# Stick-breaking attention: scores emitted two jobs ahead of their transposes, with six weight tiles and half the DMA scratch

## The chip, the core and the metric

The kernel runs on one core of a Trainium2 chip. A core has engines that run side by side, each with its own queue of instructions: PE (matrix products and transposes), DVE (element by element work and scans), ACT (activations and copies with a cast), POOL and SP (here mostly issues of transfers). The metric is the device time of one execution in microseconds, lower is better. The kernel has a median of 2229.0 us over three runs (2228.58 to 2229.59).

## The reference, cut to what matters

Two layers, each with two mixers on the same projected input; stick-breaking attention is the first of them. The rest (normalisation, compressed, selected and window attention, gates, output projection) is left out here.

```python
SEQ = 1024; DEPTH = 2; HEAD_DIM = 64; SB_HEADS = 8; Q_BLOCK = 128

def stick_breaking_attention(q, k, v):
    B, S, H, d = q.shape
    scale = d ** -0.5
    qh, kh, vh = (a.transpose(0, 2, 1, 3) for a in (q, k, v))
    outs = []
    for i in range(S // Q_BLOCK):
        t0, t1 = i * Q_BLOCK, (i + 1) * Q_BLOCK
        z = jnp.einsum('bhqd,bhkd->bhqk', qh[:, :, t0:t1], kh[:, :, :t1]).astype(jnp.float32) * scale
        strict = jnp.arange(t1)[None, :] < jnp.arange(t0, t1)[:, None]
        log_keep = jnp.where(strict, jax.nn.log_sigmoid(-z), 0.0)
        between = lax.cumsum(log_keep, axis=3, reverse=True) - log_keep
        w = jnp.where(strict, jnp.exp(jax.nn.log_sigmoid(z) + between), 0.0)
        outs.append(jnp.einsum('bhqk,bhkd->bqhd', w.astype(v.dtype), vh[:, :, :t1]))
    return jnp.concatenate(outs, axis=1)

# in the layer
a = stick_breaking_attention(heads(sb_q, SB_HEADS), heads(sb_k, SB_HEADS), heads(sb_v, SB_HEADS))
a = a.reshape(B, S, SB_WIDTH) * jax.nn.silu(sb_z)
y = jax.nn.sigmoid(m_a) * (a @ w_proj_a) + jax.nn.sigmoid(m_b) * (b @ w_proj_b)
return x + gate[:, None] * (y @ w_out)
```

## The kernel before

A layer runs `early` (projections that everything needs), then queues the remaining projections as a reserve of matrix products (`queue_projections`, the "fill"), then the sparse attention (`nsa`), then the stick-breaking stage `sb`, then what is left of the fill, then `output`. What the fill holds during `sb` are products for the gates: PE rows on lines 194, 196 and 198 with `proj` as their output, whose weights come from HBM as `raw` and are split into two parts `w` by ACT and DVE (lines 136, 137).

`sb(l)` goes over 8 heads, and in each over 4 jobs m = 0 to 3. Job m takes two tiles of 128 query rows, tile i = 2m + x with x = 0 and 1, against the first (i + 1) x 128 keys. So the widths are 128 and 256 for m = 0, 384 and 512 for m = 1, 640 and 768 for m = 2, 896 and 1024 for m = 3.

A job has a part A and a part B.

- Part A (`sb_scores`): for each chunk of up to 512 keys PE computes scores (lines 872, 873, and 875 for the mask), ACT makes C (the sigmoid of the negative score, line 1245) and E (the sigmoid of the score, line 1246), and after the last chunk DVE runs a reverse product scan over C (line 1249) and multiplies E by it (line 1250). E is then the tile of weights. Its pool has four buffers, C has three. POOL sets the border column of C.
- Part B (`pipeline`): PE transposes the two E tiles block by block (line 885, output `tr`), ACT casts the transposed block to `wh` (line 136), DVE takes the rest `wl` (line 137), and PE multiplies both with V into `av` (lines 904 and 905), three steps behind the transposes. At its end `merge` adds two halves (ACT `mt`, line 922; DVE `o`, line 923), and for odd heads `finish_pair` multiplies `o` with the gate (line 913) and stores it to AD in HBM (line 914).

`run_jobs` interleaves the pieces of part A of one job with those of part B of the job before. After each piece it pumps fill products worth a number of microseconds: `sb_us` = (1.34, 2.87, 4.77, 6.04) for the B job's m, in the first iteration, which has no B, `start_us` = 3.0. On each engine the emitted instructions are then ordered by a list scheduler, which follows the emission with small shifts, and each engine works through its own list in that order.

`load(head)` brings k (two transfers on SP's queue), V and q (on ACT's queue) into pools of two buffers. It is called at the beginning of B of (head - 1, 0). After `sb` the function `output` loads AD with transfers on POOL's queue (line 1339, three for each half of the rows; `actlo`, then split into `acthi`) and gates `gt` (line 1405). GpSimd's transfers keep their descriptors in a reserved part of SBUF, `dynamic_dma_scratch_size`, 16384 bytes of each partition where nothing is said.

Of the kernel before, what the change touches and what calls it, by code (L numbers as in the profile page):

```python
# [10 lines left out]
F32 = mybir.dt.float32  # L11
# [9 lines left out]
P = 128  # L21
S = 1024
# [65 lines left out]
class Trunk:  # L88
# [195 lines left out]
            self.run_gen(self.fill.pop(0)[1])  # L284
        self.debt = 0.0

    def run_jobs(self, jobs):


        for n in range(len(jobs) + 1):  # L290
            B = jobs[n - 1][1] if n else []
            A = jobs[n][0] if n < len(jobs) else []
            us = jobs[n - 1][2] if n else self.start_us
            merged = []
            for x in range(max(len(A), len(B))):
                merged += A[x:x + 1] + B[x:x + 1]
            for f in merged:
                f()
                self.pump(us * (1 - self.tail) / len(merged))
            self.pump(us * self.tail)  # L300
# [75 lines left out]
    def mod_ab(self, l, pool, steps):  # L376
# [3 lines left out]
        sc = self.sc  # L380
        B = self.tl(self.lay, [P, KD], F32, "Bcol", bufs=2)
        A = self.tl(self.lay, [P, KD], F32, "Acol", bufs=2)
        ab, gn = self.vectors(pool, l)
        self.mods[l] = (A, B)

        def fin(part, ps):
# [3 lines left out]
            else:  # L390
                nc.vector.tensor_tensor(B, ps, ab[:, 0], ALU.add)

# [58 lines left out]
    def norm_first(self):  # L451
# [3 lines left out]
        with tc.tile_pool(name="norm0", bufs=1, reuse_waits="tile") as pool:  # L455
            A = self.tl(self.lay, [P, KD], F32, "Acol", bufs=2)
            B = self.tl(self.lay, [P, KD], F32, "Bcol", bufs=2)
            ada = {}
# [724 lines left out]
    def sb(self, l):  # L1183
        tc, nc = self.tc, self.nc
        with tc.tile_pool(name=f"sb{l}", bufs=2, reuse_waits="tile") as pool:
            qkv = {}

            def load(head):
                if head >= 8:
                    return  # L1190
                k = self.load_stack_k(pool, 512 + head * 64)
                v = self.load_v(pool, head)
                q = self.tl(pool, [P, S], F32R, "q")
                for hl in range(2):
                    nc.scalar.dma_start(q[hl * 64:hl * 64 + 64].bitcast(F32), self.QK[hl, head * 64:head * 64 + 64, :])
                qkv[head] = (q, k, v)

            def job(head, m, st):
                hs = {}
                A, B = [], []  # L1200
                for x in range(2):
                    A += self.sb_scores(pool, m, x, lambda: qkv[head], hs)

                def begin():
                    if m == 0:
                        load(head + 1)
                    hs["ps"] = self.tl(self.pav, [P, 512], F32, "av", bufs=1)
                bursts = self.pipeline(pool, self.av_stages(pool, m, lambda: (hs["e", 0], hs["e", 1]),
                                                            lambda: qkv[head][2]), lambda: hs["ps"], True)
                B.append(lambda: (begin(), bursts[0]()))  # L1210
                B += bursts[1:]

                def fin():
                    if head % 2 == 0:
                        st[m] = self.tl(pool, [P, 256], F32, f"o{m}", bufs=1)
                    self.merge(pool, hs["ps"], st[m], head % 2)
                    if head % 2 == 1:
                        self.finish_pair(pool, st[m], head // 2 * 128, m, 512 + head // 2 * 128)
                B.append(fin)
                return A, B, self.sb_us[m]  # L1220

            load(0)
            jobs = []
            st = {}
            for head in range(8):
                for m in range(4):
                    jobs.append(job(head, m, st))
            self.run_jobs(jobs)

    def sb_scores(self, pool, m, x, qkv, hs):  # L1230

        nc = self.nc
        i = 2 * m + x
        nk = (i + 1) * P

        def chunk(c0):
            q, k, _ = qkv()
            if c0 == 0:
                hs["e", x] = self.tl(pool, [P, S], F32, "E", bufs=4)
                hs["c", x] = self.tl(pool, [P, S + 8], F32, "C", bufs=3)  # L1240
                nc.gpsimd.memset(hs["c", x][:, nk:nk + 1], 1.0)
            e, c = hs["e", x], hs["c", x]
            c1 = min(nk, c0 + 512)
            ps = self.scores(q[:, i * P:i * P + P], k, c0, c1, [(i * P, "m_strict")] if c1 == nk else [])
            nc.scalar.activation(c[:, c0:c1], ps, AF.Sigmoid, scale=-(HD ** -0.5))  # L1245
            nc.scalar.activation(e[:, c0:c1], ps, AF.Sigmoid, scale=HD ** -0.5)
            if c1 == nk:
                rev = c[:, nk - 1::-1]
                nc.vector.tensor_tensor_scan(rev, rev, rev, 1.0, ALU.mult, ALU.bypass)  # L1249
                nc.vector.tensor_tensor(e[:, 0:nk], e[:, 0:nk], c[:, 1:nk + 1], ALU.mult)  # L1250

        return [lambda c0=c0: chunk(c0) for c0 in range(0, nk, 512)]
# [206 lines left out]
```

## Time and profile before

| what | before |
|---|---|
| median of three runs | 2229.0 us (2228.58 to 2229.59) |
| time of the profiled execution | 2227.61 us |
| its span | 2225.8 us |
| PE busy | 2124.4 us (95%) |
| DVE busy | 1573.0 us (71%) |
| ACT busy | 1129.9 us (51%) |
| stick-breaking stage of layer 0, layer 1 | about 690 to 950 us, 1780 to 2040 us |

The span is the time between the first and the last instruction that the profile shows; the execution's own time is 1.8 us more. Busy time is the time in which an engine had an instruction in work; matmuls on PE are pipelined and their ends are modelled. In the waits an instruction stands with the engine that released it and the idle time ahead of it.

### The profile page before, as it was taken

What the parts mean: (1) busy time and instruction counts of PE and PEld (TensorE: products, weight loads), DVE (VectorE), ACT (ScalarE), POOL (GpSimd) and SP (SyncE); (2) the same over time, 40 slices, a digit from 0 to 9 for tenths busy, and PEclk for the clock granted to TensorE, in tenths of its full rate; (3) what the DMA queues carried; (4) which work ended last, traced back from release to release, by engine and by line L of the source; (5) the groups of instructions that cost most, each with busy time, mean ns of one, the idle gap of its engine ahead of it and who ended that gap; (6) DMA issues with size and microseconds to landing.
All of it is one profiled execution on the core that took longest, in us unless ns stands there. A gap on an engine that the chain in (4) does not pass through costs nothing.

```text
span 2225.8 us, 36846 instructions
## 1 busy us (share of the span) xinstructions
PE 2124.4 (95%) x13128; PEld 1833.5 (82%) x13128; DVE 1573.0 (71%) x3722; ACT 1129.9 (51%) x2489; POOL 73.0 (3%) x242
## 2 busy tenths in 40 slices
PE   4999999999999999999999998999999999999999
PEld 3898778988887777779889986889898877777899
DVE  5768558868765877886766852887788487787643
ACT  4433147656565655663433421665666465656410
POOL 2200000000000000010011000000000000001000
PEclk8999999999999999999999999999999999999999
DMA  7545852253116445275555355222522364534443
GB/s 287 113 136 189 251 154 81 91 152 94 64 48 159 128 130 129 81 245 177 164 151 161 107 192 141 90 90 82 146 92 68 97 151 113 146 98 166 148 124 104
DMA packets 254104, 297.05 MB, mean 133 GB/s; under 512 B 38888, under 2 KB 201568, under 8 KB 253920
## 3 DMA queue, kind: packets, MB, share of 16 engines
q1 hardware_dynamic: 213152, 250.65, 37.4%
q10 hardware_dynamic: 36224, 29.37, 5.1%
q0 software_dynamic: 4544, 14.68, 2.3%
q8 instruction: 103, 1.69, 0.3%
q14 instruction: 81, 0.66, 0.1%
HBM read 206.28 MB, written 83.89 MB: 130 GB/s over the span
## 4 chain that ended last, share of the span: by engine, by line
PE 66%; DVE 18%; DMA 7%; issue 4%; ACT 3%; POOL 1%; SPq 0%; ACTq 0%; DVEq 0%; POOLq 0%
PE proj L194 15%; PE proj L198 15%; PE proj L196 15%; PE tr L885 5%; DVE C L1249 4%; PE av L905 4%; PE av L904 3%; PE sc L872 3%; PE sc L873 3%; DVE wl L137 3%; DMA ada<-in_ada_w 2%; DVE E L1250 2%; DVE w L137 2%; DMA q<-QK 1%; DMA actlo<-AD 1%
## 5 line engine op out<-in xcount | busy, mean ns | idle before, releaser
L194 PE MATMUL proj<-acthi,w 128*128 128x512 f32 x1312 | 537.6, 410 | 3.0 <-ACT acthi L136 2.2
L196 PE MATMUL proj<-actlo,w 128*128 128x512 f32 x1312 | 538.0, 410 | 0.0
L198 PE MATMUL proj<-acthi,w 128*128 128x512 f32 x1312 | 537.2, 409 | 0.0
L136 ACT CAST w<-raw 128x512 fp32r<-128x512 f32 (+1 forms) x296 | 183.3, 623 | 227.3 <-PE proj L198 129.7
L194 PEld LDWEIGHTS proj<-acthi,w 128*128 128x128 f32 x1312 | 250.2, 191 | 43.6 <-ACT acthi L136 2.7
L137 DVE TENSOR_TENSOR wl<-tr,wh 128x512 fp32r<-128x512 f32 (+2 forms) x432 | 257.0, 611 | 40.7 <-ACT wh L136 38.3
L196 PEld LDWEIGHTS proj<-actlo,w 128*128 128x128 f32 x1312 | 250.0, 191 | 38.1 <-DVE actlo L137 0.8
L198 PEld LDWEIGHTS proj<-acthi,w 128*128 128x128 f32 x1312 | 249.6, 190 | 37.1 <-DVE w L137 0.2
L137 DVE TENSOR_TENSOR w<-raw,w 128x512 fp32r<-128x512 f32 (+1 forms) x296 | 202.5, 689 | 81.9 <-ACT w L136 80.6
L136 ACT CAST wh<-tr 128x512 fp32r<-128x512 f32 (+2 forms) x432 | 221.3, 527 | 76.4 <-PE tr L885 71.3
L194 PE MATMUL proj<-w,acthi 128*128 128x256 f32 (+1 forms) x768 | 221.5, 289 | 5.4 <-DVE s L137 2.4
L905 PE MATMUL av<-wl,V 128*128 128x256 f32 (+1 forms) x864 | 217.6, 285 | 7.6 <-DVE wl L137 7.4
L198 PE MATMUL proj<-w,actlo 128*128 128x256 f32 (+1 forms) x768 | 221.1, 288 | 0.0
L196 PE MATMUL proj<-w,acthi 128*128 128x256 f32 (+1 forms) x768 | 220.0, 286 | 0.0
L904 PE MATMUL av<-wh,V 128*128 128x256 f32 (+1 forms) x864 | 216.7, 271 | 1.2 <-DVE o L923 0.5
L1249 DVE TENSOR_TENSOR_SCAN C<-C 128x128 f32<-128x128 f32 (+7 forms) x128 | 172.7, 1350 | 55.0 <-ACT C L1245 54.5
L885 PE MATMUL tr<-ident,E 128*128 128x128 f32 x1152 | 187.4, 276 | 24.2 <-DVE E L1250 23.4
L885 PEld LDWEIGHTS tr<-ident,E 128*128 128x128 f32 x1152 | 139.1, 140 | 68.1 <-DVE E L1250 35.4
L905 PEld LDWEIGHTS av<-wl,V 128*128 128x128 f32 x864 | 162.7, 188 | 31.0 <-DVE wl L137 19.7
L872 PE MATMUL sc<-kk,q 128*128 128x512 f32 (+3 forms) x512 | 176.8, 346 | 8.8 <-DVE mx L1085 4.1
L873 PE MATMUL sc<-kk,q 128*128 128x512 f32 (+3 forms) x512 | 175.5, 343 | 0.0
L904 PEld LDWEIGHTS av<-wh,V 128*128 128x128 f32 x864 | 163.0, 189 | 13.7 <-ACT wh L136 3.6
(247 smaller groups left out, 3902.8 us busy)
## 6 DMA issues: line engine op xcount, KB each, us to landing
raw<-in_w_in SPq DMA_DIRECT2D x168, 256.0 KB, 3.0
ada<-in_ada_w SPq DMA_DIRECT2D x48, 512.0 KB, 5.1
kk<-QK SPq DMA_DIRECT2D x48, 512.0 KB, 8.6
q<-QK ACTq DMA_DIRECT2D x64, 256.0 KB, 4.2
QK<-s SPq DMA_DIRECT2D x32, 512.0 KB, 3.0
MD<-sz SPq DMA_DIRECT2D x64, 256.0 KB, 2.5
QK<-s SPq DMA_DIRECT2D x48, 256.0 KB, 3.9
VD<-s SPq DMA_DIRECT2D x48, 256.0 KB, 2.0
```

The costliest lines, as they stand in the source:

```text
L136: nc.scalar.copy(hi, src)
L137: nc.vector.tensor_tensor(lo, src, hi.bitcast(F32), ALU.subtract)
L194: nc.tensor.matmul(ps, lh, rh, start=(x == 0), stop=False)
L196: nc.tensor.matmul(ps, lh, rl, start=False, stop=False)
L198: nc.tensor.matmul(ps, ll, rh, start=False, stop=(x == n - 1))
L872: nc.tensor.matmul(ps, q, k[:, 0, c0:c1], start=True, stop=False)
L873: nc.tensor.matmul(ps, q, k[:, 1, c0:c1], start=False, stop=not masks)
L885: nc.tensor.transpose(pt[:, x * P:x * P + P], b, self.ident)
L904: nc.tensor.matmul(ps[:, c:d], lhsT, hi[:, a:b], start=(first and x == 0), stop=False, skip_group_check=True)
L905: nc.tensor.matmul(ps[:, c:d], lhsT, lo[:, a:b], start=False, stop=(last and x == n - 1), skip_group_check=True)
L1249: nc.vector.tensor_tensor_scan(rev, rev, rev, 1.0, ALU.mult, ALU.bypass)
L1250: nc.vector.tensor_tensor(e[:, 0:nk], e[:, 0:nk], c[:, 1:nk + 1], ALU.mult)
```

## The change

`run_jobs` gets a distance `far`, 1 as a default and 2 for the stick-breaking stage: part A of job n is interleaved with part B of job n - 2. The pumped amount follows the B job, and `start_us` is pumped in the first two iterations. E has six buffers. The next head's `load` goes from the beginning of B of (head, 0) to the end of A of (head, 1). The reserved scratch is 8192 bytes a partition instead of 16384, which leaves room for two more E tiles of 4096 bytes a partition.

```diff
-    def run_jobs(self, jobs):
+    def run_jobs(self, jobs, far=1):
-        for n in range(len(jobs) + 1):
-            B = jobs[n - 1][1] if n else []
+        for n in range(len(jobs) + far):
+            B = jobs[n - far][1] if n >= far else []
             A = jobs[n][0] if n < len(jobs) else []
-            us = jobs[n - 1][2] if n else self.start_us
+            us = jobs[n - far][2] if n >= far else self.start_us
...
                 for x in range(2):
                     A += self.sb_scores(pool, m, x, lambda: qkv[head], hs)
+                if m == 1:
+                    A.append(lambda: load(head + 1))
                 def begin():
-                    if m == 0:
-                        load(head + 1)
                     hs["ps"] = self.tl(self.pav, [P, 512], F32, "av", bufs=1)
...
-            self.run_jobs(jobs)
+            self.run_jobs(jobs, 2)
...
-                hs["e", x] = self.tl(pool, [P, S], F32, "E", bufs=4)
+                hs["e", x] = self.tl(pool, [P, S], F32, "E", bufs=6)
...
-    nc = bacc.Bacc("TRN2", target_bir_lowering=False, num_devices=1)
+    nc = bacc.Bacc("TRN2", target_bir_lowering=False, num_devices=1, dynamic_dma_scratch_size=8192)
```

Line numbers from `sb` on are one higher in the changed kernel (the scan is line 1250, the product 1251).

DVE in a middle head of layer 0, before: the rows from the second E of m = 1 to the second E of m = 2 (the scan over C is named SCALAR_TENSOR_TENSOR here; the last number is the width, which tells the tile). B of m = 0 ends with the first o, and wl_9297 and wl_9315 belong to B of m = 1.

```order
L1250 TENSOR_TENSOR E_9254<-E_9254,C_9255 128x512
L923 TENSOR_TENSOR o_1900_8907<-av_9244,mt_9271 64x256
L913 TENSOR_TENSOR o_1900_8907<-o_1900_8907,szl_9274 128x256
L137 TENSOR_TENSOR wl_9297<-tr_9291,wh_9296 128x512
L1249 SCALAR_TENSOR_TENSOR C_9281<-C_9281 128x640
L137 TENSOR_TENSOR wl_9315<-tr_9310,wh_9314 128x384
L1250 TENSOR_TENSOR E_9280<-E_9280,C_9281 128x640
L1249 SCALAR_TENSOR_TENSOR C_9321<-C_9321 128x768
L923 TENSOR_TENSOR o_1917_8981<-av_9290,mt_9349 64x256
L1250 TENSOR_TENSOR E_9320<-E_9320,C_9321 128x768
```

DVE in a middle head of layer 0, of the change: from the split of B of m = 0 (wl_9659) to the first scan of m = 3. wl_9716 belongs to B of m = 1.

```order
L137 TENSOR_TENSOR wl_9659<-tr_9654,wh_9658 128x384
L1250 SCALAR_TENSOR_TENSOR C_9646<-C_9646 128x640
L1251 TENSOR_TENSOR E_9645<-E_9645,C_9646 128x640
L923 TENSOR_TENSOR o_2081_9686<-av_9653,mt_9687 64x256
L1250 SCALAR_TENSOR_TENSOR C_9678<-C_9678 128x768
L1251 TENSOR_TENSOR E_9677<-E_9677,C_9678 128x768
L137 TENSOR_TENSOR wl_9716<-tr_9710,wh_9715 128x512
L1250 SCALAR_TENSOR_TENSOR C_9701<-C_9701 128x896
```

The scans of 640 and 768 stood behind the first split of B of m = 1, and now stand ahead of it, behind the split of B of m = 0.

PE at the first transposes of B of m = 1, before: scores of A of m = 2 (sc_9283), gate products, and the transposes of the two E tiles of m = 1. E_9254 is the first row of DVE's piece above.

```order
L872 MATMUL sc_9283<-kk_8872,q_8877 128x512
L873 MATMUL sc_9283<-kk_8872,q_8877 128x512
L198 MATMUL proj_9221<-acthi_26_135,w_8484 128x512
L194 MATMUL proj_9221<-acthi_26_135,w_8484 128x512
L885 MATMUL tr_9291<-ident_85,E_9224 128x128
L885 MATMUL tr_9291<-ident_85,E_9254 128x128
```

PE at the same transposes, of the change: the scores ahead of them are now of m = 3 (sc_9703), and E_9523 and E_9548 are the two tiles of m = 1, which DVE writes ahead of wl_9659, the first row of its second piece above.

```order
L872 MATMUL sc_9703<-kk_9199,q_9204 128x512
L873 MATMUL sc_9703<-kk_9199,q_9204 128x512
L194 MATMUL proj_9610<-acthi_28_137,w_8987 128x512
L885 MATMUL tr_9710<-ident_85,E_9523 128x128
L885 MATMUL tr_9710<-ident_85,E_9548 128x128
```

The transposes stood beside the scores one job on, and now stand beside those two jobs on.

## Rows read from the trace of the kernel before

**Rows 1.** the page's part 1: busy us, share of the span, instructions
```profile
span 2225.8 us, 36846 instructions
...
PE 2124.4 (95%) x13128; PEld 1833.5 (82%) x13128; DVE 1573.0 (71%) x3722; ACT 1129.9 (51%) x2489; POOL 73.0 (3%) x242
```

**Rows 2.** waits, 690 to 960 us (layer 0): total, times, longest
```profile
PE tr L885 <- DVE E L1250: 11.5, 19, 1.1
...
PE av L905 <- DVE wl L137: 3.7, 10, 0.7
```

**Rows 3.** waits, 1775 to 2045 us (layer 1)
```profile
PE tr L885 <- DVE E L1250: 11.9, 19, 1.1
```

**Rows 4.** timeline of PE: start us, duration us, instruction, idle before
```profile
861.37 0.40 PE L194 MATMUL proj<-acthi,w 128*128 128x512 f32 x1
861.61 0.27 PE L885 MATMUL tr<-ident,E 128*128 128x128 f32 x1
...
862.17 0.48 PE L198 MATMUL proj<-acthi,w 128*128 128x512 f32 x1
863.38 0.88 PE L885 MATMUL tr<-ident,E 128*128 128x128 f32 x6 [0.73 <-DVE E L1250]
```

**Rows 5.** window 860 to 893: length, busy us of PE, PEld, DVE, ACT, POOL
```profile
860.00:893.00 33.00, 31.41 (x181) 25.68 (x180) 26.22 (x36) 18.95 (x44) 0.89 (x9) 1.00 0.49 134
```

**Rows 6.** timeline of DVE, one head of layer 0
```profile
860.32 0.68 DVE L137 TENSOR_TENSOR w<-raw,w 128x512 fp32r<-128x512 f32 x1
...
863.57 1.48 DVE L1249 TENSOR_TENSOR_SCAN C<-C 128x640 f32<-128x640 f32 x1
865.19 0.82 DVE L1250 TENSOR_TENSOR E<-E,C 128x640 f32<-128x640 f32 x1
866.05 1.16 DVE L137 TENSOR_TENSOR wl<-tr,wh 128x512 fp32r<-128x512 f32 x2
867.12 1.75 DVE L1249 TENSOR_TENSOR_SCAN C<-C 128x768 f32<-128x768 f32 x1
869.00 0.96 DVE L1250 TENSOR_TENSOR E<-E,C 128x768 f32<-128x768 f32 x1
869.99 0.43 DVE L923 TENSOR_TENSOR o<-av,mt 64x256 f32<-64x256 f32 x1
...
871.36 0.69 DVE L137 TENSOR_TENSOR wl<-tr,wh 128x512 fp32r<-128x512 f32 x1 [0.49 <-ACT wh L136]
871.97 2.02 DVE L1249 TENSOR_TENSOR_SCAN C<-C 128x896 f32<-128x896 f32 x1
874.12 1.09 DVE L1250 TENSOR_TENSOR E<-E,C 128x896 f32<-128x896 f32 x1
...
876.19 2.28 DVE L1249 TENSOR_TENSOR_SCAN C<-C 128x1024 f32<-128x1024 f32 x1
```

**Rows 7.** waits of PE, 726.6 to 925.2 us: six middle head cycles
```profile
PE tr L885 <- DVE E L1250: 7.2, 12, 1.0
PE av L905 <- DVE wl L137: 2.7, 7, 0.7
PE av L904 <- DVE o L923: 0.3, 1, 0.3
```

**Rows 8.** timeline of POOL, end of layer 1's stage
```profile
2038.00 2.14 POOL L1405 DMA_DIRECT2D gt<-MD  x4 [11.36 <-PE av L905]
```

**Rows 9.** timeline of PE, end of layer 1's stage
```profile
2051.29 0.79 PE L194 MATMUL proj<-acthi,w 128*128 128x512 f32 x1 [2.23 <-ACT acthi L136]
```

**Rows 10.** the page's part 3: GpSimd's DMA queue: packets, MB, share
```profile
q0 software_dynamic: 4544, 14.68, 2.3%
```

**Rows 11.** timeline of DVE, another head of layer 0
```profile
805.18 0.69 DVE L137 TENSOR_TENSOR wl<-tr,wh 128x512 fp32r<-128x512 f32 x1 [0.92 <-ACT wh L136]
```

**Rows 12.** line 1339's loads: issue to landing
```profile
DMA to landing us min/median/max: 3.7/8.0/12.3
```

## The prediction

> **What bounds the kernel now.** I read the page's first part, then the waits of each stick-breaking stage, then one head's rows on DVE and PE. PE is busy 2124.4 of 2225.8 us, DVE 1573.0 [rows 1]: PE sets the time, so an edit counts only by the gaps that it takes out of PE's stream or puts in. In the first layer's stage PE waits 11.5 us in 19 pieces for E before a transpose and 3.7 us in 10 pieces for a wl before line 905 [rows 2]. The second layer's stage has 11.9 in 19 for E [rows 3], and for wl the first layer's row once more. A gap costs more than its number, since a matmul's modelled end overlaps the next start: a gate product that began at 861.37 lasts 0.40, and the transpose behind it began 0.24 after it did: ends overlap by 0.16, and a gap hides as much. At 862.17 to 863.38 one sees it: 1.21 us between two starts, 0.73 of them shown as idle [rows 4]. So 58 waits cost 30.8 shown and 58 x 0.16 = 9.3 unseen: 40 us in both layers, 11.9 + 11.5 + 38 x 0.16 = 29.5 of them for E.
>
> Why there, when DVE has room? In 860 to 893, one head, DVE works 26.2 of 33 us [rows 5]. But the work comes bunched in the long scans and the products that make E of them. From start to start: scan 640 1.62, its E 0.86; scan 768 1.88, its E 0.99; scan 896 2.15, its E 1.0; scan 1024 itself 2.28, some 2.4 to its E, and that about 1.2 by its columns [rows 6]. Beside them stand the short B parts, which bring PE little to do.
>
> **The change part by part.** PE, DVE and ACT issue the same instructions with the same shapes, so no engine gains or loses work. What moves is the partner (A2 is a head's scores of m=2, B0 its transposes and products of m=0, and so on): A2 ran beside B1 and now runs beside B0, A3 beside B1 instead of B2, the next head's A0 beside B2, its A1 beside B3.
>
> *E waits.* A transpose now reads an E made a whole iteration earlier. I take all 38 E waits out: -29.5 us. Below that they can't go, and above by a few leftovers.
>
> *The wl waits.* DVE works in the order written, and in it a wl stands behind whatever scans were emitted before it. Before, wl_9297 of B1 stands ahead of scan 640. Now wl_9716 of B1 stands behind scan 640, E, the merge's o, scan 768 and E, as both order pieces show. What lies between wl_9659 (B0) and the end of wl_9716 on DVE: 1.62 + 0.86 + about 0.4 for o + 1.88 + 0.99 + 0.69 for wl = 6.4 us [rows 6]; 6.1 if each step is the shortest that I find for its kind. PE goes in that time from line 904 on wh_9658 to line 905 on wl_9716: 9 gate products at 0.235, three of them 0.09 longer behind a mask or a transpose (2.4), three score pairs of 512 columns (0.47 each), pairs of 256 and 384 with masks (0.7), seven transposes (0.6), five av products (0.4): 5.5 us, with the step of [rows 4] scaled by columns. The split wl_9659 itself ends some 0.4 behind line 904's start. So PE stands for 0.4 + 6.1 - 5.5 = 1.0, and up to 1.3. I go on in the same way. wl_9739 comes behind scan 896: 2.4 on DVE against 1.9 of PE work, 0.5. wl_9800 of B2 comes behind E 896, scan 1024, o, E 1024, scan and E 128: 6.1 against 5.9, 0.2. wl_9824 behind scan 256: 1.2 against 1.05, 0.2. From there DVE has caught up. The first line 904 of B0 waits about 0.4 for its cast, because PE comes to it soon after its transposes. Sum for a head without extras: 2.2 to 2.3.
>
> In that stretch of DVE there is no slack, so each further row lengthens a wait: line 913 of odd heads, as large as the merge's o, about 0.33 each in such a queue, and a split w of weights 0.6 each (0.43 and 0.68 on their own [rows 6]). By the order the six middle cycles hold three of the first and five of the second in it, and one E 128 falls behind its wl (-0.25): 6 x 2.2 + 1.0 + 3.0 - 0.25 = 16.9 us for the cycles of heads 1 to 6. The same cycles of before, from the 384 scan of head 1 to that of head 7, lose 7.2 + 2.7 + 0.3 in 20 gaps [rows 7] and 20 x 0.16, 13.4. Net +3.5 a layer.
>
> *The ends of the stage.* There are two iterations without a B at the start, not one, and `start_us` is spent in both; the last two have no A. I lay these out with the same steps: start 5.6 us of gaps against 4.4, last head 3.9 against 3.3, +1.8 a layer. This is the weakest part; 0 to +4 is its bound.
>
> *The load moved.* It leaves B(head,0)'s begin for the end of A(head,1); before, these stood in one iteration. In the new order it comes an iteration's part later beside B(head-1,3), still two iterations ahead of its first reader, 12 us or more. At nothing; its cover is these two iterations. V's transfer is issued on ACT's queue and waits there for PE's last reader, just ahead of the merge's copy that waits for the same PE rows, so nothing behind it is held longer.
>
> *The stage's last stretch in layer 1.* POOL waits 11.4 us for PE's last av product, issues four gt loads in 2.1 and then the loads of AD [rows 8]; PE then waits 2.2 for acthi [rows 9] after 48 gate products that cover the loads. Now 40 of those stand behind the last av, since 8 went ahead: 1.9 less cover. But POOL's second gt now waits for an av five rows before the last, so about 1.3 comes back: +0.6.
>
> *The halved scratch.* No instruction changes. POOL's queue moved 4544 packets in the whole run, 284 for each of 16 engines [rows 10]; the loads in flight at one time are a fraction of that, and four are issued in 2.1 us without a wait [rows 8]. I take nothing; its upper bound is rival 3.
>
> Sum: 2 x (3.5 + 1.8) + 0.6 = +11.2 us. The profiled execution took 2227.6, 1.8 over its span and 1.4 under the median; 2229.0 + 11.2 gives **2240 us**.
>
> Bounds: if the wl waits stay as they are, -29.5, 2199.5. If nothing of DVE's delay in the first two pairs is covered by what PE has in them, a head loses what DVE has more than PE in the pairs (A2,B0) and (A3,B1): by the steps above DVE 5.35 for A2 and 1.0 for B0's wl and o, 6.8 and 1.65 for A3 and B1, 14.8 in all; PE 3.5 and 6.5, by the products that the order sets there. That is 4.8 instead of the 2.2: 2.6 more for 14 heads, 36 over the sum, about 2276.
>
> **The rivals.**
> 1. *Faster: DVE gets ahead of PE.* Before, a part of the E wait is a round trip: E, transpose, ACT's cast, and DVE idles 0.92 before its wl at 805.18 [rows 11]. Without it, DVE runs through. If A2's scan 640 begins 1.5 us earlier than I laid it, while B3's av products still run, the stalls of 1.0, 0.5 and 0.2 vanish and a head loses 0.5 where I have 2.2. For it: DVE has some 7 us of room in a head [rows 5]. Against it: the order puts A2's first score behind nine products after B3's last av, so DVE can't begin earlier than ACT gets it. From the forecast that is 14 x 1.7 = 24 us and most of the 3.7 of extras a layer: about 2212; half of it gives 2226.
> 2. *No change.* The wl waits come to 2.2 a head for the 2.2 that goes, the w splits fall where DVE has room, the ends cancel: 2227 to 2232.
> 3. *Slower by POOL.* If the smaller scratch lets only one load be in flight, each of the four groups of three AD loads, now issued back to back, waits for landings, two of 8 us (the median [rows 12]) in each group. Layer 1's last stretch has little else to cover it: 16 us there, some 10 in layer 0, with the rest as forecast about 2265. The Trainium skill, "DMA: Bandwidth & Descriptors", section "SWDGE vs HWDGE vs iDMA", says that GpSimd's own DMAs are written as descriptors into rings that live in a reserved part of SBUF, so a smaller one could hold POOL back; no run here shows such a wait as yet. Against it is the small count of packets.
>
> **How the numbers follow.** Forecast (slower by 4 to 25 us): 0.52, rivals 1, 2 and 3: 0.24, 0.2, 0.04. What a measurement can tell from no change is 0.2%, 4.5 us. The forecast's own range is 2232 to 2254. The terms are sums of short steps, each stall a difference of two of them: 0.3 us more or less at each of 14 heads is 4, and wrong cover for the w splits another 6. Rival 2 lies between, and I take in rival 1 as far as 2215, short of its middle; rival 3 and a forecast gone to its bound stay out: 2215 to 2254. Faster 0.24, same 0.2, slower 0.56.
>
> **What would show it.** In the profile after: PE's E waits before transposes under 3 us in all (23.4 now); line 905's wl waits three to five times their 3.7 a layer, the longest behind scan 768 or 896; DVE without idle from scan 640 to E 1024; the middle heads' period, from 384 scan to 384 scan, half a microsecond longer; the first and last heads longer; PE's wait for acthi in layer 1 near 3. I am wrong if line 905 waits under 8 us a layer (rival 1), or if POOL's rows stand apart by several us with PE waiting for acthi (rival 3).

## The result, and the profile after

The changed kernel takes 2258.8 us (median of 4 runs, 2256.81 to 2261.8) against 2229.3 of before in the same job: ratio 1.0137, 95% interval 1.0124 to 1.015. It is slower, as forecast, but by 29.5 us where 11 were forecast, and outside the range (2215 to 2254).

The page of the changed kernel, its first part and the three groups of part 5 that answer to [rows 1 to 3] (busy us, mean ns | idle us ahead, what ended most of it):

```profile
span 2255.0 us, 36875 instructions
...
PE 2135.5 (95%) x13128; PEld 1838.2 (82%) x13128; DVE 1569.1 (70%) x3722; ACT 1127.4 (50%) x2489; POOL 72.3 (3%) x242
...
L905 PE MATMUL av<-wl,V 128*128 128x256 f32 (+1 forms) x864 | 221.3, 289 | 30.4 <-DVE wl L137 30.2
L904 PE MATMUL av<-wh,V 128*128 128x256 f32 (+1 forms) x864 | 219.8, 272 | 6.4 <-DVE o L923 3.2
...
L885 PE MATMUL tr<-ident,E 128*128 128x128 f32 x1152 | 180.3, 274 | 3.3 <-DVE E L1251 2.9
```

The E waits (PE ahead of a transpose, for DVE's E) fell from 23.4 to 2.9 us over both layers, the wl waits (PE ahead of line 905) rose from 7.4 to 30.2. That is the exchange that was forecast. One head of layer 0, DVE of the changed kernel, the stretch in which the forecast laid out its waits:

```profile
872.11 0.56 DVE L137 TENSOR_TENSOR wl<-tr,wh 128x384 fp32r<-128x384 f32 x1 [2.70 <-ACT wh L136]
872.58 1.48 DVE L1250 TENSOR_TENSOR_SCAN C<-C 128x640 f32<-128x640 f32 x1
874.19 0.83 DVE L1251 TENSOR_TENSOR E<-E,C 128x640 f32<-128x640 f32 x1
875.05 0.43 DVE L923 TENSOR_TENSOR o<-av,mt 64x256 f32<-64x256 f32 x1
875.51 1.76 DVE L1250 TENSOR_TENSOR_SCAN C<-C 128x768 f32<-128x768 f32 x1
877.18 0.40 DVE L913 TENSOR_TENSOR o<-o,szl 128x256 f32<-128x256 f32 x1
877.50 0.95 DVE L1251 TENSOR_TENSOR E<-E,C 128x768 f32<-128x768 f32 x1
878.49 0.69 DVE L137 TENSOR_TENSOR wl<-tr,wh 128x512 fp32r<-128x512 f32 x1
879.09 2.01 DVE L1250 TENSOR_TENSOR_SCAN C<-C 128x896 f32<-128x896 f32 x1
881.03 0.53 DVE L137 TENSOR_TENSOR wl<-tr,wh 128x384 fp32r<-128x384 f32 x1
```

And what PE did at the two wl of these rows:

```profile
879.23 0.38 PE L905 MATMUL av<-wl,V 128*128 128x256 f32 x1 [0.93 <-DVE wl L137]
879.46 0.28 PE L904 MATMUL av<-wh,V 128*128 128x256 f32 x1
879.57 0.28 PE L905 MATMUL av<-wl,V 128*128 128x256 f32 x1
...
880.75 0.28 PE L904 MATMUL av<-wh,V 128*128 128x256 f32 x1
881.61 0.39 PE L905 MATMUL av<-wl,V 128*128 128x256 f32 x1 [0.59 <-DVE wl L137]
881.84 0.22 PE L904 MATMUL av<-wh,V 128*128 128x128 f32 x1
```

From 872.11 on DVE has no idle time. The wl that starts at 878.49 stands behind two scans and their products, and PE waits 0.93 us for it, and 0.59 for the next, which stands behind scan 896; forecast were 1.0 and 0.5. The middle heads' period was forecast from one 384 scan to the next. The first and the last of seven in layer 0 (changed kernel, then before):

```profile
726.05 0.94 DVE L1250 TENSOR_TENSOR_SCAN C<-C 128x384 f32<-128x384 f32 x1
...
927.68 0.96 DVE L1250 TENSOR_TENSOR_SCAN C<-C 128x384 f32<-128x384 f32 x1 [2.03 <-ACT C L1246]
```

```profile
726.60 0.96 DVE L1249 TENSOR_TENSOR_SCAN C<-C 128x384 f32<-128x384 f32 x1 [0.51 <-ACT C L1245]
...
925.24 0.96 DVE L1249 TENSOR_TENSOR_SCAN C<-C 128x384 f32<-128x384 f32 x1 [2.11 <-ACT C L1245]
```

Six cycles take 201.63 us against 198.64: 0.5 us more a head, 3.0 a layer, where 3.5 was forecast. But this stretch is cut at rows of DVE, and PE has less to do in it than before: 414 gate products for 423 and two score products less, all missing from the first of the six cycles (61 gate products for 71). Cut at PE's own rows, from the first `av` product of head 1 to that of head 7, the work is nearly the same (422 gate products for 420, two score products less; changed kernel, then before):

```profile
737.01 0.28 PE L904 MATMUL av<-wh,V 128*128 128x256 f32 x1
...
939.92 0.39 PE L904 MATMUL av<-wh,V 128*128 128x256 f32 x1 [0.28 <-ACT wh L136]
```

```profile
729.10 0.39 PE L904 MATMUL av<-wh,V 128*128 128x256 f32 x1 [0.26 <-DVE o L923]
...
926.13 0.28 PE L904 MATMUL av<-wh,V 128*128 128x256 f32 x1
```

These six heads take 202.91 us for 197.03, and 203.05 for 197.11 in layer 1: 1.0 us more a head, 5.9 a layer. So the middle heads lost more than was forecast, and more time is lost behind them. The next table cuts both profiles at instructions that both have: the last transpose of `cpg` (sparse attention) in a layer, the last `av` product, the first product on `yh` (output), the end of PE's work. The last column is the number of gate products between that transpose and the last av, a layer, as the order lists them.

| us | up to cpg, layer 0 | stage 0 | last av to yh | to cpg, layer 1 | stage 1 | last av to yh | to the end | products |
|---|---|---|---|---|---|---|---|---|
| before | 592.9 | 360.0 | 46.1 | 682.5 | 356.0 | 93.8 | 90.3 | 751 |
| changed | 596.6 | 368.9 | 50.0 | 684.3 | 365.0 | 95.5 | 90.6 | 759 |

Stage and what follows it grew by 12.8 and 10.7 us (8.9 + 3.9, 9.0 + 1.7); the middle heads hold 5.9 of each. The other 5.5 lie where both kernels have the same instructions in the same order; between all the profiles shown here the first column alone goes from 592.5 to 600.8, whatever the kernel. The other columns scatter too: x1_scratch and x2_near below, as fast as before, have 357.2 and 358.2 for stage 0 and 45.9 and 48.7 for what follows it, so 2 to 3 us between two single profiles of this table show little.

POOL's rows around the stage's end, before and changed, layer 0:

```profile
939.93 2.10 POOL L1339 DMA_DIRECT2D actlo<-AD  x3 [5.87 <-PE proj L196]
947.34 2.15 POOL L1405 DMA_DIRECT2D gt<-MD  x4 [5.32 <-ACT w L136]
951.38 1.50 POOL L1339 DMA_DIRECT2D actlo<-AD  x2 [1.89 <-PE proj L198]
```

```profile
946.28 1.53 POOL L1340 DMA_DIRECT2D actlo<-AD  x2 [3.31 <-PE proj L196]
958.64 0.57 POOL L1340 DMA_DIRECT2D actlo<-AD  x1 [10.83 <-DMA AD<-o]
963.76 2.14 POOL L1406 DMA_DIRECT2D gt<-MD  x4 [4.55 <-PE tr L885]
965.90 1.50 POOL L1340 DMA_DIRECT2D actlo<-AD  x2
977.76 0.56 POOL L1340 DMA_DIRECT2D actlo<-AD  x1 [10.36 <-issue]
```

Before, the first four gate loads went out 5.6 us ahead of the last av product (952.9); now 1.7 (965.4). The third load of AD stands ahead of them and waits 10.8 us for a store, but it does not set their time: behind it POOL idles 4.55 us more, by the profile for a transpose on PE. And x2_near, which has all of the change but the distance, sends its gates 1.7 us ahead of the last av product too (952.6), with its three loads of AD back to back:

```profile
939.67 2.10 POOL L1340 DMA_DIRECT2D actlo<-AD  x3 [5.91 <-PE proj L196]
950.88 2.15 POOL L1406 DMA_DIRECT2D gt<-MD  x4 [9.11 <-ACT acthi L136]
```

In the changed kernel PE then waits at 979.63, since ACT's cast of a weight stands behind the activation of a fifth gate (ACT, then PE):

```profile
977.93 0.63 ACT L1408 ACTIVATE gt<-gt 128x512 f32<-128x512 f32 x1 [5.35 <-DMA gt<-MD]
```

```profile
979.63 0.80 PE L194 MATMUL proj<-acthi,w 128*128 128x512 f32 x1 [3.17 <-ACT w L136]
980.23 0.63 PE L196 MATMUL proj<-actlo,w 128*128 128x512 f32 x1
980.66 0.63 PE L198 MATMUL proj<-acthi,w 128*128 128x512 f32 x1
```

This gate was issued on SP's queue, at 971.49, 6.1 us behind the last av product, and landed 6.4 us later. Before, it was issued 7.5 us behind that product (960.39) and landed after 3.5. Why it took longer is not shown.

### The profile page after: what moved, and what is told of

The parts are those of the page before. It is cut to its first block, busy times and chain, and to the rows that moved or that the text cites. A ratio compares the mean times of both kernels' runs of the same rounds, so it can differ in the third digit from the quotient of the medians.

```text
span 2255.0 us, 36875 instructions
## 1 busy us (share of the span) xinstructions
PE 2135.5 (95%) x13128; PEld 1838.2 (82%) x13128; DVE 1569.1 (70%) x3722; ACT 1127.4 (50%) x2489; POOL 72.3 (3%) x242
## 4 chain that ended last, share of the span: by engine, by line
PE 65%; DVE 18%; DMA 6%; issue 5%; ACT 4%; POOL 1%; SPq 0%; ACTq 0%; DVEq 0%; POOLq 0%
PE proj L194 15%; PE proj L198 15%; PE proj L196 15%; PE tr L885 5%; DVE C L1250 4%; PE av L905 4%; PE av L904 3%; PE sc L872 3%; PE sc L873 3%; DVE E L1251 3%; DVE wl L137 3%; DVE w L137 1%; DMA q<-QK 1%; DMA gt<-MD 1%; DVE o L923 1%
## 5 line engine op out<-in xcount | busy, mean ns | idle before, releaser
L905 PE MATMUL av<-wl,V 128*128 128x256 f32 (+1 forms) x864 | 221.3, 289 | 30.4 <-DVE wl L137 30.2
L885 PE MATMUL tr<-ident,E 128*128 128x128 f32 x1152 | 180.3, 274 | 3.3 <-DVE E L1251 2.9
```

The source lines that it names most:

```text
L885: nc.tensor.transpose(pt[:, x * P:x * P + P], b, self.ident)
L905: nc.tensor.matmul(ps[:, c:d], lhsT, lo[:, a:b], start=False, stop=(last and x == n - 1), skip_group_check=True)
```

## The experiments

All are compared with before by the ratio of their medians in one job (five rounds).

| run | distance | what differs | median us | ratio (95%) |
|---|---|---|---|---|
| x1_scratch | 1 | half the scratch alone | 2230.1 | 0.9999 (0.9988 to 1.001) |
| x2_near | 1 | six tiles, scratch, moved load | 2229.6 | 0.9996 (0.9986 to 1.0006) |
| x3_fill | 2 | amounts moved to the pairs short of PE work | 2247.8 | 1.008 (1.0066 to 1.0093) |
| x4_bfirst | 2 | part B emitted ahead of part A | 2250.1 | 1.0092 (1.0077 to 1.0107) |
| x7_end | 2 | distance one for the last jobs | 2259.2 | 1.0136 (1.0118 to 1.0153) |
| x6_start | 2 | `start_us` halved | 2257.5 | 1.0127 (1.0111 to 1.0143) |
| x8_end_fill | 2 | x7_end and x3_fill | 2252.4 | 1.0115 (1.0098 to 1.0132) |
| x5_near_fill | 1 | amounts moved | 2213.7 | 0.9932 (0.9917 to 0.9946) |
| x9_near_keep | 1 | amounts moved, sum 14.3 for 15.0 | 2205.5 | 0.9892 (0.988 to 0.9905) |
| x10_far_keep | 2 | x3_fill, sum 14.3 | 2235.9 | 1.0034 (1.0021 to 1.0047) |
| x11_far_bfill | 2 | x3_fill and x4_bfirst | 2238.1 | 1.0034 (1.0022 to 1.0046) |
| x12_near_bfill | 1 | x5_near_fill, B ahead of A | 2249.7 | 1.0084 (1.0069 to 1.01) |
| x13_far_bkeep | 2 | x10_far_keep, B ahead of A | 2220.2 | 0.9964 (0.9951 to 0.9977) |
| x14_near_more | 1 | amounts moved, sum 13.3 | 2214.6 | 0.9933 (0.992 to 0.9947) |
| x15_near_old_keep | 1 | old proportions, sum 14.3 | 2236.8 | 1.0038 (1.0025 to 1.005) |
| x16_far_old_keep | 2 | old proportions, sum 14.3 | 2247.8 | 1.0087 (1.0073 to 1.0101) |

The same cuts of the profiles as above:

| us | up to cpg, layer 0 | stage 0 | last av to yh | to cpg, layer 1 | stage 1 | last av to yh | to the end | products |
|---|---|---|---|---|---|---|---|---|
| x1_scratch | 599.2 | 357.2 | 45.9 | 684.8 | 356.0 | 92.5 | 90.4 | 751 |
| x2_near | 594.4 | 358.2 | 48.7 | 682.8 | 355.9 | 91.6 | 90.5 | 751 |
| x3_fill | 595.2 | 364.5 | 50.7 | 684.6 | 361.4 | 97.7 | 90.6 | 768 |
| x4_bfirst | 596.8 | 362.2 | 49.4 | 684.7 | 362.5 | 97.0 | 90.5 | 759 |
| x5_near_fill | 592.5 | 350.6 | 48.1 | 685.1 | 346.8 | 94.0 | 90.3 | 766 |
| x6_start | 597.6 | 369.5 | 49.6 | 685.9 | 367.6 | 93.4 | 90.6 | 753 |
| x7_end | 594.9 | 368.0 | 49.8 | 684.8 | 366.8 | 94.9 | 90.5 | 765 |
| x9_near_keep | 596.0 | 344.8 | 48.3 | 682.0 | 343.9 | 92.8 | 90.4 | 745 |
| x10_far_keep | 596.9 | 359.0 | 51.1 | 682.3 | 354.1 | 96.2 | 90.5 | 754 |
| x13_far_bkeep | 600.8 | 353.7 | 49.7 | 685.9 | 349.0 | 92.7 | 90.6 | 753 |
| x14_near_more | 596.7 | 338.2 | 61.5 | 684.5 | 334.3 | 104.0 | 90.4 | 704 |
| x16_far_old_keep | 595.4 | 367.2 | 50.2 | 681.5 | 363.5 | 92.5 | 90.4 | 748 |

The profile of x13_far_bkeep is of its longest execution (2228.3 us, 8 over its median).

**Is it the distance, or what came with it?**

```diff
x1_scratch, against before:
-    nc = bacc.Bacc("TRN2", target_bir_lowering=False, num_devices=1)
+    nc = bacc.Bacc("TRN2", target_bir_lowering=False, num_devices=1, dynamic_dma_scratch_size=8192)
x2_near, against the changed kernel:
-            self.run_jobs(jobs, 2)
+            self.run_jobs(jobs)
```

> The kernel before with half the DMA scratch and nothing else. Theory A (the distance of two jobs costs the time: wl splits behind bunched scans, and a stage end with less left to cover the loads of AD): 2229, within 2 us of before. Theory B (the smaller scratch holds POOL's transfers back, since its loads of AD in the changed kernel stand 10.8 and 10.4 us apart): 2238 or more, with POOL's three loads apart here too.

> The changed kernel with the distance back at one job; six E tiles, the moved load and the halved scratch stay. Theory A: 2229 within 4 us, E waits near 23 us again and line 905's wl waits near 7. Theory B, or a cost of the moved load: 2236 or more.

Neither differs from before by what can be measured. x1_scratch issues POOL's three loads of AD back to back, and x2_near has PE's E waits at 11.8 us a layer and its wl waits at 2.9 (before 11.7 and 3.7). So rival 3 (POOL held back by the scratch) falls, the moved load costs nothing that shows in the time, and the whole 29 us belong to the distance. One thing in x2_near is not as before: its gates go out late in layer 0, and what follows the stage there takes 48.7 us for 46.1. That comes with the six tiles or the moved load, for x1_scratch has neither (gates 5.5 us ahead of the last av product, 45.9).

**Are the wl waits a matter of PE's cover or of DVE's order?**

```diff
x3_fill, against the changed kernel:
-        self.sb_us = (1.34, 2.87, 4.77, 6.04)
+        self.sb_us = (4.8, 5.7, 1.9, 2.6)
x4_bfirst, against the changed kernel (distance two alone):
-                merged += A[x:x + 1] + B[x:x + 1]
+                merged += B[x:x + 1] + A[x:x + 1]
```

> The changed kernel with the pumped gate products given to the iterations in which DVE has more to do than PE: sb_us (4.8, 5.7, 1.9, 2.6) for (1.34, 2.87, 4.77, 6.04), the same sum. Theory A: the wl waits of 30 us in both layers fall under 8 and the time to 2230 to 2238, since the stage's ends stay as they are. Theory C (a wl waits for its place in DVE's queue however much PE has to do): wl waits over 20 us, 2250 or more.

> The changed kernel with each piece of part B emitted ahead of the piece of part A that it is paired with, in the stick-breaking stage. Theory A: some splits come ahead of a scan in DVE's queue, the wl waits fall by a third to two thirds of 30 us: 2240 to 2250. Theory C' (the list scheduler undoes it, or the casts on ACT become the wait): 2255 to 2262.

> The changed kernel with both part B ahead of part A (x4_bfirst) and the moved amounts (x3_fill). If a wl's place in DVE's queue and PE's cover are two parts of one cost, wl waits under 8 us in both layers: 2232 to 2242. If both already took the same part of it: 2244 to 2250.

Each wins: 11 and 9 us. Both together come to 2238.1, 21 us under the changed kernel: they add up. PE's waits in x3_fill, layer 0's stage (700 to 955), where the changed kernel has 13.4 for wl:

```profile
PE av L905 <- DVE wl L137: 8.5, 16, 1.3
PE av L904 <- DVE o L923: 3.1, 2, 2.8
PE tr L885 <- DVE wl L137: 2.5, 2, 1.9
```

The wl waits fell from 30.2 to 17.1 us over both layers, not under the 8 that were expected, and waits for o and for the transposes' buffer came up. x3_fill missed its range by 10 us, also because its stretch behind the stage did not get shorter (50.7 and 97.7) although 9 more products had been drawn ahead of the last av; at 0.234 us each they lengthen the stage by 2.1.

x4_bfirst, at the edge of its range, won its 9 us without the mechanism that was expected of it. Its wl waits did not fall by a third or more; over both layers they rose to 33.1:

```profile
L905 PE MATMUL av<-wl,V 128*128 128x256 f32 (+1 forms) x864 | 221.7, 290 | 33.7 <-DVE wl L137 33.1
```

They became fewer and longer. Layer 0's middle heads (first av product of head 1 to that of head 7), the changed kernel, then x4_bfirst (total, times, longest):

```profile
PE av L905 <- DVE wl L137: 11.1, 19, 1.3
```

```profile
PE av L905 <- DVE wl L137: 11.8, 12, 2.1
```

With all kinds of waits it is 12.4 us in 24 and 12.0 in 13, and the six heads take 199.6 us for 202.9. So a wait costs more than its length, and the number of waits counts. x11_far_bfill came out in its range with 20.2 us of wl waits over both layers, not the under 8 that was expected.

**Is the rest lost at the stage's end?**

```diff
x7_end, against the changed kernel:
-        for n in range(len(jobs) + far):
+        N = len(jobs)
...
+            seq = [(n, n - 2) for n in range(N - 3)] + [(N, N - 5)] + [(n, n - 1) for n in range(N - 3, N + 1)]
+        for n, b in seq:
...
x6_start, against the changed kernel:
-            us = jobs[n - far][2] if n >= far else self.start_us
+            us = jobs[n - far][2] if n >= far else self.start_us / far
```

> The changed kernel, but the distance goes back to one job for the last three jobs of a stage: B of (6,3) gets an iteration without a part A, and from there the stage ends as in the kernel before. Theory D (a good part of the 29 us is lost at the stage's end, since its last two iterations have no part A and the store that the loads of AD wait for comes closer to the end): 2242 to 2250, with PE's waits after the last av product in both layers as in the kernel before. Theory A alone (all is lost by wl in the middle heads): 2255 to 2260.

> The changed kernel with start_us halved, so that the two iterations without a part B together pump as much as the single one before; some 13 gate products a layer move from the start to the end. If the end is short of products to cover its loads: 2250 to 2255. If these products only move the waits: 2256 to 2261.

> The end of x7_end and the pumped amounts of x3_fill together. If end and middle are separate costs, the two gains add up: 2230 to 2238, and with E waits under 5 us and wl waits under 15 the stage could come out level with before. If they share a cause: 2242 to 2248.

My theory of the end (D) fell. With the last three jobs at distance one the time is the same (2259.2), and both stretches behind the stage stay long (49.8 and 94.9). The edit keeps two iterations without a part A, though, and only moves one of them ahead of the last three jobs, so it doesn't show what such an iteration costs. Halving `start_us` shortens the stretch behind the stage by 0.4 and 2.1 us and lengthens the stage itself by 0.6 and 2.6. It also moves what stands beside what in the middle heads, which took 205.1 us for 202.9 with four gate products less, so it is no clean test of the ends either. x8_end_fill is no better than x3_fill, and above both of its ranges.

**Is it the amount of cover, at either distance?** By the same reckoning as for x3_fill (DVE's work of a pair of parts less PE's), the pairs of the kernel before are short of cover too.

```diff
x5_near_fill, x9_near_keep, x14_near_more, x15_near_old_keep, against before:
-        self.sb_us = (1.34, 2.87, 4.77, 6.04)
+        self.sb_us = (3.7, 4.6, 5.3, 1.3)
+        self.sb_us = (3.5, 4.4, 5.2, 1.2)
+        self.sb_us = (3.3, 4.1, 5.0, 0.9)
+        self.sb_us = (1.24, 2.7, 4.56, 5.8)
x10_far_keep and x13_far_bkeep, then x16_far_old_keep, against the changed kernel:
-        self.sb_us = (1.34, 2.87, 4.77, 6.04)
+        self.sb_us = (4.6, 5.5, 1.8, 2.4)
+        self.sb_us = (1.24, 2.7, 4.56, 5.8)
```

> The kernel before, distance one, with the pumped products given by the same reckoning to the iterations in which DVE has more to do: sb_us (3.7, 4.6, 5.3, 1.3), the same sum. If the amount of PE work beside DVE's bunches decides, and not the distance: 2208 to 2222, E waits of 23 us halved. If the E waits are the round trip from DVE over PE and ACT: 2226 to 2232.

> x5_near_fill with a little less pumped in each head, sb_us (3.5, 4.4, 5.2, 1.2), 0.7 us less: some 24 gate products a layer stay for the end of the stage. If the end is short of products to cover its loads, as the stretch from the last av product to the first product on yh says (about 5 us longer at equal products in x5_near_fill): 2204 to 2211. If the middle loses what the end gains: 2212 to 2217.

> x3_fill (distance two) with sb_us (4.6, 5.5, 1.8, 2.4), 0.7 us less a head, so that products stay for the end. End short of products: 2234 to 2243. Middle loses as much: 2245 to 2250.

> x5_near_fill with part B ahead of part A, distance one. At this distance the splits already stand ahead of the long scans, and a transpose needs the E of the job just before, which comes later in the order then: 2213 to 2222. If the order only helps: 2205 to 2211.

x5_near_fill is 16 us faster than before with four numbers changed and distance one. Its E waits and wl waits over both layers, from part 5 of its page:

```profile
L905 PE MATMUL av<-wl,V 128*128 128x256 f32 (+1 forms) x864 | 216.7, 285 | 1.7 <-DVE wl L137 1.5
...
L885 PE MATMUL tr<-ident,E 128*128 128x128 f32 x1152 | 180.7, 275 | 8.2 <-DVE E L1250 7.4
```

So two thirds of the E waits at distance one were not a round trip that only a longer distance can hide; they were PE running out of other work. x9_near_keep, which leaves some products for the end, is the fastest of all, 2205.5. x10_far_keep wins 12 us over x3_fill by the same step. x12_near_bfill shows the other side of the order: at distance one, B ahead of A brings the E waits of layer 0 back to 15.8 us. It loses 36 us to x5_near_fill, far more than was expected.

> Distance two with part B ahead of part A, moved proportions and the reserve: sb_us (4.6, 5.5, 1.8, 2.4). If the three gains add up (9, 11 and 12 us of 29 were seen one at a time or together): 2222 to 2230. If order and amounts share one cost: 2231 to 2238. In no theory does it reach x9_near_keep's 2205.

> x9_near_keep with a further 1.0 us less pumped a head, sb_us (3.3, 4.1, 5.0, 0.9). If the end still lacks cover (its stretch did not get shorter in x9_near_keep): 2198 to 2204. If the middle now lacks it: 2206 to 2212.

> The kernel before with its own proportions scaled to the same sum as x9_near_keep: sb_us (1.24, 2.7, 4.56, 5.8). If the reserve helps whatever the proportions: 2219 to 2225. If the first jobs are too short of products already: 2228 to 2234.

> The changed kernel with the old proportions scaled to the same sum: sb_us (1.24, 2.7, 4.56, 5.8). If a good part of the 29 us is products pumped too early for the end (two iterations of start_us): 2244 to 2252. If the reserve takes from the starved first pairs what it gives to the end: 2255 to 2262.

With order, proportions and reserve, distance two comes to 2220.2, 8 us under before, and stays 15 above x9_near_keep. Its wl waits are still 17.6 us, and its E waits are gone:

```profile
L905 PE MATMUL av<-wl,V 128*128 128x256 f32 (+1 forms) x864 | 221.3, 290 | 18.9 <-DVE wl L137 17.6
...
L885 PE MATMUL tr<-ident,E 128*128 128x128 f32 x1152 | 181.8, 274 | 0.5 <-DVE E L1251 0.4
```

x13_far_bkeep lies just under its range. x14_near_more goes past the best reserve, and past both of its ranges: its stage is 338.2 us, but the stretch behind it 61.5. The two controls are the surprise: the reserve alone makes before slower by 8 us (x15_near_old_keep, above both ranges; its E waits grow to 14.8 in layer 0) and the changed kernel faster by 11 (x16_far_old_keep), though its wl waits stay at 32.4 over both layers.

## Why the prediction was wrong, point by point

- **PE bounds the time: right.** DVE is busy 70% of the changed kernel's span too, PE 95%. That a wait costs more than it shows is right as well, and x4_bfirst bears it out.
- **E waits out, -29.5: right in kind, a little less.** 2.9 us remained, all in the first jobs, where nothing is ahead.
- **The wl waits of the middle heads, +3.5 a layer: right in kind, too small; the first step that failed.** They stand where they were forecast, 0.93 and 0.59 against 1.0 and 0.5, and x2_near shows that the distance makes them. By the forecast's own reckoning (what is shown, and 0.16 a wait) layer 0's six heads lose 12.4 + 24 x 0.16 = 16.2 us, where 16.9 was forecast, and before 9.9 + 19 x 0.16 = 12.9: 3.3 more. But the six heads grew by 5.9 at nearly the same work. The price of a wait was too low: behind 22 of the changed kernel's waits, and 7 before, the next av product starts 0.22 us after the waiting one instead of 0.12, some 1.5 us. About 1 us a layer is in steps that I can't place.
- **The ends of the stage, +1.8 a layer, "0 to +4": inside the bound.** The stages without these six heads grew by 3.0 and 3.1 us. Six more gate products stand in them, which is 1.4 (8 more stand ahead of the last av, 759 for 751, two of them in the middle heads), and PE's shown waits there rose by 1.3 in layer 0.
- **The last stretch, nothing in layer 0 and +0.6 in layer 1: the second step that failed.** I looked for a wait of PE as in [rows 9] in layer 1 and took layer 0 to be free since it had none. The stretches grew by 3.9 and 1.7 us with 8 fewer products in them, so the products drawn forward gave nothing back: 5.8 and 3.5 at equal products. In layer 0 PE waits 3.17 us behind a fifth gate that landed late. 2.6 of the 3.9 stand in x2_near too, so they are not the distance's alone. In layer 1 the three kernels at distance one with the old amounts go from 91.6 to 93.8, so the 1.7 is known to 2 us at best. There PE waited in other places than the forecast's acthi: 4.2 us for actlo at 2085.65. The cause stays open: POOL's wait for the store of AD is not it in layer 0, for x16_far_old_keep issues its three loads back to back, and its stretch is still 3.4 us longer than before's at equal products (50.2 for 46.1, with 3 products more).
- **The scratch and the load at nothing: right in the time**, by x1_scratch and x2_near.
- **Rival 1, DVE ahead of PE:** it did not come. x13_far_bkeep reaches something like it, but only with changed order and amounts.
- **Rival 3, POOL:** its sign came, loads 10.8 and 10.4 us apart, and x1_scratch shows that the scratch is not the reason.

Of the 29.5 us the table places 23.5 in the stages and behind them: 11.8 in the middle heads (7.0 forecast), 6.1 in the ends of the stages (3.6), 5.6 behind (0.6). The rest lies within what such profiles scatter by. x16_far_old_keep wins back 11 us by pumping 0.7 us less a head, without fewer wl waits, so an amount pumped too early belongs to the loss; its profile places 6 of these in the stages and behind them (1.7, 1.5 and 3.0, less 0.2), the rest in stretches with the same instructions. How the loss divides between the amounts and the order of DVE's queue is not settled.

## What to carry to other kernels

Emitting a producer further ahead of its consumer removes the wait that one sees only if the engine between them has nothing else in its queue that a nearer consumer needs: here the splits stood behind the scans, and the wait changed its name. To see what a change cost, cut the trace at rows of the engine that bounds the time, and count the work between the cuts: cut at DVE's rows, nearly half of the middle heads' loss was hidden by work, nine gate products above all, that had moved out. Before lengthening a distance, work out for each pair of parts what the two engines have to do, and move the filler to the pairs in which the slower one is ahead; four numbers gave 1.1% (x9_near_keep) where the distance took 1.4%. And look at what covers the loads after a stage before drawing its filler forward.

## What was not expected of the hardware

After PE's wait of 3.17 us the granted clock fell. In the windows of the changed kernel (length, busy of PE, PEld, DVE, ACT and POOL, granted clock, DMA share, GB/s):

```profile
979.63:983.50 3.87, 3.87 (x10) 3.02 (x11) 3.17 (x5) 2.35 (x5) 0.00 (x0) 0.57 0.44 140
983.50:991.00 7.50, 7.50 (x34) 5.87 (x32) 4.95 (x9) 4.38 (x9) 0.00 (x0) 1.00 0.48 154
```

The products there begin 0.43 us apart (980.23 to 980.66) instead of 0.23: the lower of the two levels, 1.2 GHz, for most of that stretch. Ten of them take 3.87 us, where ten steps of 0.23 are 2.3: 1.6 more, half as much again as the wait. I had no term for this. The kernel before has one such stretch too, behind its wait of 2.23 us in layer 1 [rows 9]:

```profile
2051.29:2055.00 3.71, 3.71 (x9) 2.71 (x10) 3.71 (x7) 3.34 (x7) 0.34 (x1) 0.56 0.41 155
```

The changed kernel has them in both layers (granted clock 0.58 in 2085.65 to 2089.50, behind the 4.2 us). Over whole runs its mean granted clock was 0.986 to 0.989, that of before 0.990 to 0.993 in the experiments' jobs; but x6_start had 0.990 to 0.991 and was as slow (2257.5 us), so the clock alone does not set the time. A shorter effect goes with each wl wait shown here: the av product behind the waiting one begins 0.23 us after it (879.23 to 879.46), not 0.11 as further on (879.46 to 879.57).
